# Step-wise delta-rule preparation inside the projection, and float32 attention on halves of the TensorE columns

## The chip, the cores and the metric

One core of a Trainium2 chip runs the whole program. The metric is device time in microseconds (us), the median of several executions. TensorE is the matrix engine (PE; PEld is its weight load), VectorE is DVE, ScalarE is ACT, GpSimd is POOL; SP issues most DMAs.

## The reference, cut to what matters

A two-layer decoder trunk takes 1024 prompt tokens and 8 x 8 sample tokens (1088 columns in all). The change is in layer 0, whose mixer has two parts behind one input projection:

```python
qkv, z, b_raw, a_raw, cq, ckv, kpe = jnp.split(h @ w_in, SPLIT_AB, axis=-1)
qkv = jax.nn.silu(sum(ext[:, i:i + t] * conv_w[i] for i in range(CONV_W)))
q = l2norm(q); k = l2norm(k)
o_a, s_new = gated_delta_rule(q, k, v, g, beta, s0)          # 4 heads of 128
o_b = attend(q_nope, q_pe, ckv, kpe, w_uk, w_uv)             # 8 heads
return jnp.concatenate([o_a, o_b], -1) @ w_out, new_buf, s_new, ckv, kpe
```

Per chunk of tokens and head the delta rule needs the products k k^T and k q^T times a decay, the inverse of a unit triangular matrix made of the first, and then a recurrence over chunks. Attention of the sample tokens reads 4096 cached positions for each of 8 sequences through a page table; attention of the prompt is causal over 1024 positions. Afterwards come the layer's MLP, an HGRN2 layer and a second MLP, which the change does not touch.

## The kernel before, in words

Activations lie as 128 features x 1088 columns, cut in three chunks of 384, 384 and 320 columns (`CH`). A projection tile is 8 contraction steps; operands are split in a high and a low float32r part and each step is three passes (`dense`, L334 to L336), so a tile is 24 passes for each chunk and 72 in all.

`in_proj` computes 21 such tiles: two of cq, one of rotary key and gates, two of ckv, then per delta-rule head the q, k and v tiles (kept with three earlier columns in `ext`, written to DRAM as `ext_d`) and z.

`attend_sample` runs beside it. For each of 4 pairs of sequences and 8 groups of 4 pages, `scores` loads the transposed latent of each sequence (`la`), splits it in high and low parts (ACT copies, DVE subtracts) and multiplies; high and low parts of the query lie in columns 0 to 63 and 64 to 127, so two halves are added afterwards (L801, L802). `mix` transposes the probabilities (L829), gathers the latent rows (`lt`, an indirect DMA that POOL issues), splits them too and multiplies (L850). A ninth small group holds the new tokens.

`prompt_prep` (32 tiles of 512 columns, two contraction steps of three passes) makes the prompt's keys, values and queries. Then `gdn_heads` runs four heads in two streams (0 and 2; 1 and 3). `ready(h)` loads `ext_d`, does the convolutions (L949, L952), SiLU, norms (L966, L969), decays (L978 to L987) and products (L996, L997), then waits until the head before is inverted, inverts its triangular matrices with 32x32 tiles (L1027) and prepares the recurrence; `recur(h)` is the recurrence (L1178 to L1197) and the output norm (L1206). `attend_prompt` is woven with it: `scores` makes softmax rows of one head and 128 queries, `mix` transposes and splits the probabilities of 256 queries and multiplies them with V, whose high and low parts fill the 128 columns (L1385), and adds the halves. When the heads are done, `out_early` takes five of the eight output-projection rows, and after attention `out_late` the rest.

The generators are merged by `weave`, which takes the stream with the least cost so far; a scheduler then orders each engine's instructions by that order as priority and by what is ready in a simulated timeline. Waits on tile buffers and on PSUM banks come from the pools: `WT`, `BK`, `BP`, `GB` and `LA` hold stream weights, bank counts and buffer counts.

Of the kernel before, what the change touches and what calls it, by code (L numbers as in the profile page):

```python
# [19 lines left out]
NT = 1088  # L20
# [15 lines left out]
def shape_constants():  # L36
# [31 lines left out]
    t = np.arange(64) % 8  # L68
    smk = np.full((128, 8, 64), 0.0, np.float32)
    for bb in range(8):  # L70
        col = np.arange(64)
        ok = (col[None, :] // 8 == bb) & (col[None, :] % 8 <= t[:, None])
        smk[:64, bb] = np.where(ok, 0.0, NEG)
# [3 lines left out]
def lay_out(I):  # L77
# [3 lines left out]
    A["cst"], A["rope"], A["rope2"], A["smk"] = c, rope, rope2, smk.reshape(128, 512)  # L81
# [55 lines left out]
    kr = f("cache_mla_krope")[0].reshape(NPOOL, 1, 2, 64, 32).transpose(0, 1, 2, 4, 3)  # L137
    kr = np.broadcast_to(kr, (NPOOL, 2, 2, 32, 64)).reshape(NPOOL, 128, 64)
# [188 lines left out]
def dense(k, acc, w, xs, kk_n, first=True, last=True):  # L327

    nc = k.nc
    wh, wl = w  # L330
    for kk in range(kk_n):
        xh, xl = xs[kk]
        f, l = first and kk == 0, last and kk == kk_n - 1
        nc.tensor.matmul(acc, wh[:, kk], xh, start=f, stop=False)  # L334
        nc.tensor.matmul(acc, wh[:, kk], xl, start=False, stop=False)  # L335
        nc.tensor.matmul(acc, wl[:, kk], xh, start=False, stop=l)  # L336

# [85 lines left out]
def in_proj(k):  # L423
# [3 lines left out]
    k.ext_d = k.dr.tile([4, 3, 128, 1115], F32, name="ext_d")  # L427
    k.z_d = k.dr.tile([4, 128, NT], F32, name="z_d")
    k.cq_d = k.dr.tile([2, 128, NT], F32, name="cq_d")
    xp_cm = k.P("xp", side="right")  # L430
# [32 lines left out]
    def tile(w, c):  # L463
        p = k.mm()
        dense(k, p[:, :CH[c][1]], w, xs[c], 8)
        return p

    def proj(evac, steps=None):
# [3 lines left out]
        for c, (t0, n) in enumerate(CH):  # L472
            p = tile(w, c)
# [158 lines left out]
    nc.sync.dma_start(cvi, A["sconv"])  # L632
    for h in range(4):
        for part in range(3):
# [14 lines left out]
            yield from proj(evac, None if k.keys_ready else two(ckvn))  # L649
# [4 lines left out]
            nc.sync.dma_start(k.ext_d[h, part], ext)  # L654
        z = E(f"z{h}")
        yield from proj(evac_to(z))
        nc.sync.dma_start(k.z_d[h], z[:, :NT])
    nc.sync.dma_start(O["conv"], cvo)
    xp_cm.__exit__(None, None, None)


GY = 3
# [3 lines left out]
def attend_sample(k):  # L666
# [8 lines left out]
    la_t = lambda name: T([128, 1280], name, tag="la", bufs=LA)  # L675
# [14 lines left out]
    cksh, cksl = T([128, 2, 64], "cksh", F32R), T([128, 2, 64], "cksl", F32R)  # L690
    ltsh, ltsl = T([64, 256], "ltsh", F32R), T([64, 256], "ltsl", F32R)
    kso = T([128, 64], "kso", F32R)
    idb, smb = T([128, 128], "idb", BF16), T([128, 8, 64], "smb", BF16)

    def own_keys():
        cks = la_t("cks")[:, 0:128].rearrange("p (l t) -> p l t", t=64)
        nc.sync.dma_start(cks, O["latn"].rearrange("l p n -> p l n")[:, :, SEQ:NT])
        split_pair(k, cksh, cksl, cks)
# [3 lines left out]
        split_pair(k, ltsh, ltsl, p[0:64, 0:256])  # L702

        k4 = la_t("k4")[:, 0:64]
        nc.gpsimd.memset(k4, 0.0)
        for j in range(2):
            nc.sync.dma_start(k4[64 * j:64 * j + 32, :], O["kpr"][:, SEQ:NT])
        nc.scalar.copy(kso, k4)
        nc.vector.tensor_tensor(kso[64:96, :], k4[64:96, :], kso[64:96, :].bitcast(F32), ALU.subtract)
        nc.vector.tensor_copy(idb, k.ident)  # L710
        sml = la_t("sml")[:, 0:512]
        nc.scalar.dma_start(sml, A["smk"])
        nc.vector.tensor_copy(smb.rearrange("p b t -> p (b t)"), sml)
# [14 lines left out]
    ql = T([128, 2, 8, 2, 64], "ql", F32R)  # L728
# [6 lines left out]
    for l in range(2):  # L735
# [3 lines left out]
        d = lambda j: ql[:, l, :, j, :].rearrange("p b (h t) -> p b h t", t=8)  # L739
        nc.scalar.copy(d(0), bht(p))  # L740
        nc.vector.tensor_tensor(d(1), bht(p), d(0).bitcast(F32), ALU.subtract)
        yield 1

    qr = T([128, 2, 8, 2, 64], "qr", F32R)
    zz = T([128, 1], "zz")
    nc.vector.memset(zz, 0.0)
# [3 lines left out]
    for a in range(2):  # L750
        for r in range(4):
            o = slice(32 * r, 32 * r + 32)
            if r % 2 == a:
                d = lambda j: qr[o, a, :, j, :].rearrange("p b (h t) -> p b h t", t=8)
                nc.scalar.copy(d(0), bht(p[o]))
                nc.vector.tensor_tensor(d(1), bht(p[o]), d(0).bitcast(F32), ALU.subtract)
            else:
                nc.scalar.copy(qr[o, a].rearrange("p b j t -> p (b j t)"), zz[o].broadcast_to([32, 1024]))
    yield 1

    flat = lambda w: w.rearrange("p a t -> p (a t)")
    Sx, mg, sg = {}, {}, {}
    held = deque(maxlen=8)

    def scores(pr, g):
# [5 lines left out]
        for j in range(2):  # L771
            b = 2 * pr + j
            p = k.sc()
            if g < 8:
                la = la_t(f"la{pr}{g}{j}").rearrange("p (i n) -> p i n", n=320)
# [3 lines left out]
                for i, pg in enumerate(pgs):  # L779
                    held.append(nc.sync.dma_start(la[:, i], A["latT"][bass.ds(pg, 1)].rearrange("o p n -> (o p) n")))  # L780
                lh = T([128, 4, 256], f"lh{pr}{g}{j}", F32R, tag="lh", bufs=LH)
                ll = T([128, 4, 256], f"ll{pr}{g}{j}", F32R, tag="ll", bufs=LH)
# [118 lines left out]
    yield 1  # L901


LA = 4
LH = 3


# [664 lines left out]
GB = [2]  # L1572
# [371 lines left out]
```

## Time and profile before

| | before |
|---|---|
| median of 3 runs | 3364.34 us (3357.28 to 3365.59) |
| the profiled execution | 3368.05 us, of which 3366.0 us are its span |
| PE, DVE, ACT, POOL busy | 3191.1, 1987.2, 1306.1, 560.3 us |
| mean granted TensorE clock | 0.967 |

The span runs from the first to the last instruction. A busy PE is one with any pass in its pipeline, whose ends are modelled: how fast it works is read from the distance of starts.

### The profile page before, as it was taken

Reading aid. Unit: us, or ns where it says so; the run is one execution under the profiler, and the core shown is the slowest. Engines: PE = TensorE matmul, PEld = TensorE weight load, DVE = VectorE, ACT = ScalarE, POOL = GpSimd, SP = SyncE. Lnnn points to the kernel's source line nnn. Section 1 sums busy time; section 2 is a strip of 40 time slices with the busy share of each in tenths; the row PEclk is TensorE's granted clock in tenths of the full one; section 3 lists DMA queues with packets and bytes.
Section 4 is the critical chain, followed back from the end, with each engine's and each line's share of the span. In section 5 each row is a group of like instructions: output and inputs, shape, how many; then the busy total and the mean of one; then the engine's idle time right before and its main releaser. Section 6 shows DMA issues by size and latency. Waiting matters only on the chain.

```text
span 3366.0 us, 63206 instructions
## 1 busy us (share of the span) xinstructions
PE 3191.1 (95%) x26180; PEld 3034.3 (90%) x26180; DVE 1987.2 (59%) x3511; ACT 1306.1 (39%) x2293; POOL 560.3 (17%) x536
## 2 busy tenths in 40 slices
PE   8999977888999999999999999999989999999997
PEld 7899966766888999999999888888879999999997
DVE  5788787667675544544455666555566444444456
ACT  5566674556453322112211544445535221122212
POOL 3022242102201100000000344544432000000002
PEclk9999988888889999999999999999989999999999
DMA  4687775022032111111111211111232111011111
GB/s 146 207 262 246 231 260 182 23 79 63 25 133 84 38 51 45 39 43 51 44 44 42 88 53 53 53 60 52 82 102 71 39 51 45 32 51 51 44 38 54
DMA packets 128687, 282.41 MB, mean 84 GB/s; under 512 B 14192, under 2 KB 76848, under 8 KB 128400
## 3 DMA queue, kind: packets, MB, share of 16 engines
q1 hardware_dynamic: 106656, 204.24, 18.3%
q10 hardware_dynamic: 12528, 40.58, 3.7%
q0 software_dynamic: 9216, 33.56, 3.2%
q8 instruction: 205, 3.36, 0.4%
q14 instruction: 82, 0.67, 0.1%
HBM read 233.42 MB, written 44.90 MB: 83 GB/s over the span
## 4 chain that ended last, share of the span: by engine, by line
PE 68%; DVE 5%; ACT 5%; POOL 3%; issue 2%; DMA 1%; SPq 0%; ACTq 0%; DVEq 0%; POOLq 0%
PE mm L335 11%; PE mm L334 11%; PE mm L336 11%; PE sm L1620 7%; PE sm L1622 7%; PE sm L1621 7%; PE po L1385 1%; PE tr L1394 1%; POOL y L1774 1%; DVE x L1770 1%; POOL y L1773 1%; DVE xl L318 1%; PE sm L1756 1%; POOL qg L1822 1%; PE sc L1359 1%
## 5 line engine op out<-in xcount | busy, mean ns | idle before, releaser
L334 PE MATMUL mm<-xh,wh 128*128 128x384 f32 (+1 forms) x2808 | 929.2, 331 | 12.5 <-ACT wh L265 11.0
L336 PE MATMUL mm<-xh,wl 128*128 128x384 f32 (+1 forms) x2808 | 926.5, 330 | 1.1 <-issue 0.9
L335 PE MATMUL mm<-xl,wh 128*128 128x384 f32 (+1 forms) x2808 | 925.6, 330 | 0.6 <-issue 0.6
L1623 DVE TENSOR_TENSOR xr<-xr,sm 128x384 f32<-128x384 f32 (+1 forms) x768 | 404.8, 531 | 433.1 <-PE sm L1622 433.0
L334 PEld LDWEIGHTS mm<-xh,wh 128*128 128x128 f32 x2808 | 530.0, 189 | 17.2 <-ACT wh L265 11.0
L336 PEld LDWEIGHTS mm<-xh,wl 128*128 128x128 f32 x2808 | 530.0, 189 | 4.8 <-issue 1.1
L335 PEld LDWEIGHTS mm<-xl,wh 128*128 128x128 f32 x2808 | 529.8, 189 | 4.3 <-issue 1.1
L1620 PE MATMUL sm<-hh,dh 128*128 128x384 f32 (+1 forms) x1536 | 504.5, 328 | 6.6 <-DVE xr L1623 5.2
L1622 PE MATMUL sm<-hh,dl 128*128 128x384 f32 (+1 forms) x1536 | 502.8, 328 | 0.0
L1621 PE MATMUL sm<-hl,dh 128*128 128x384 f32 (+1 forms) x1536 | 502.2, 327 | 0.0
L286 POOL TENSOR_TENSOR ssa<-ssa,ssq 128x384 f32<-128x384 f32 (+1 forms) x90 | 94.9, 1055 | 1751.0 <-ACT ssq L284 1748.0
L1597 ACT ACTIVATE hraw<-hraw 128x384 f32<-128x384 f32 (+1 forms) x192 | 96.9, 505 | 693.7 <-DVE hraw L1596 693.7
L1620 PEld LDWEIGHTS sm<-hh,dh 128*128 128x128 f32 x1536 | 288.6, 188 | 9.7 <-DVE xr L1623 7.5
L1621 PEld LDWEIGHTS sm<-hl,dh 128*128 128x128 f32 x1536 | 288.6, 188 | 0.5
L1622 PEld LDWEIGHTS sm<-hh,dl 128*128 128x128 f32 x1536 | 288.6, 188 | 0.0
L265 ACT CAST dh<-dr 128x1024 fp32r<-128x1024 f32 x64 | 66.9, 1048 | 385.7 <-PE sm L1621 381.2
L1596 DVE SCALAR_TENSOR_TENSOR hraw<-mm,rb 128x384 f32<-128x384 f32 (+1 forms) x192 | 102.7, 535 | 182.3 <-PE mm L336 182.2
L266 DVE TENSOR_TENSOR hl<-hraw,hh 128x384 fp32r<-128x384 f32 (+1 forms) x192 | 102.4, 533 | 114.9 <-ACT hh L265 114.9
L265 ACT CAST wh<-wr 128x1024 fp32r<-128x1024 f32 x96 | 100.6, 1048 | 122.0 <-PE mm L335 118.6
L266 DVE TENSOR_TENSOR wl<-wr,wh 128x1024 fp32r<-128x1024 f32 x96 | 121.0, 1262 | 43.0 <-ACT wh L265 43.0
L841 POOL DMA_INDIRECT lt<-in_lat,ix x64 | 70.8, 1106 | 187.4 <-DVE ltl L266 170.0
L265 ACT CAST hh<-hraw 128x384 fp32r<-128x384 f32 (+1 forms) x192 | 95.0, 495 | 5.1
(755 smaller groups left out, 5404.1 us busy)
## 6 DMA issues: line engine op xcount, KB each, us to landing
la<-in_latT SPq DMA_DIRECT2D x256, 160.0 KB
wr<-in_w_up SPq DMA_DIRECT2D x64, 512.0 KB
dr<-in_w_down ACTq DMA_DIRECT2D x64, 512.0 KB
wr<-in_w_in_c SPq DMA_DIRECT2D x32, 512.0 KB
win<-in_w_in_ab SPq DMA_DIRECT2D x21, 512.0 KB
ext_d<-ext SPq DMA_DIRECT2D x12, 557.5 KB
oC_d<-g SPq DMA_DIRECT2D x8, 544.0 KB
q_d<-q SPq DMA_DIRECT2D x16, 256.0 KB
```

The source lines that it names most:

```text
L265: k.nc.scalar.copy(hi, src)
L266: (eng or k.nc.vector).tensor_tensor(lo, src, hi.bitcast(F32), ALU.subtract)
L286: nc.gpsimd.tensor_tensor(acc, acc, t, ALU.add)
L334: nc.tensor.matmul(acc, wh[:, kk], xh, start=f, stop=False)
L335: nc.tensor.matmul(acc, wh[:, kk], xl, start=False, stop=False)
L336: nc.tensor.matmul(acc, wl[:, kk], xh, start=False, stop=l)
L1596: nc.vector.scalar_tensor_tensor(raw[:, s], p[:, :n], 0.0, k.rb[:, s], ALU.max, ALU.mult)
L1597: nc.scalar.activation(raw[:, s], raw[:, s], AF.Square)
L1620: nc.tensor.matmul(p[:, :n], wh[:, m], hh[:, s], start=a, stop=False)
L1621: nc.tensor.matmul(p[:, :n], wh[:, m], hl[:, s], start=False, stop=False)
L1622: nc.tensor.matmul(p[:, :n], wl[:, m], hh[:, s], start=False, stop=b)
L1623: nc.vector.tensor_tensor(k.xr[c][:, m], k.xr[c][:, m], p[:, :n], ALU.add)
```

## The change

Three parts. First, convolutions, SiLU, norms, decays and key products of each head are made during `in_proj`: two generators, `conv` and `pairs`, are put in a queue, and after contraction steps 2, 4 and 7 of every chunk (`RK`) one step of the queue is emitted. The results (`y_d`, `U_d`, `A_d`) go to DRAM in place of `ext_d`, and `ready` loads them and begins at the inversion. Second, sample attention multiplies the cached latents as float32, without splits: the two sequences of a pair use array columns 0 to 63 and 64 to 127. Third, prompt attention works on head pairs: the two heads' values fill the two halves of the columns, the probabilities are float32 and copied from PSUM once, by ACT and DVE in turn. Scores of prompt attention keep the three passes.

```diff
-def dense(k, acc, w, xs, kk_n, first=True, last=True):
+def dense(k, acc, w, xs, kk_n, first=True, last=True, between=None):
...
+        if between:
+            between(kk)
...
+    def between(kk):
+        if kk in RK:
+            step()
...
+    def conv(h, part, e, y):
+        w = lambda i: k.vec[:, V_CW + 4 * (4 * part + h) + i:V_CW + 4 * (4 * part + h) + i + 1]
+        es, ys = b11(e[:, 1027:1115]), b8(y[:, SEQ:NT])
+        nc.scalar.mul(y[:, :SEQ], e[:, 0:SEQ], w(0))
+        nc.scalar.mul(ys, es[:, :, 0:8], w(0))
+        for i in range(1, 4):
+            nc.vector.scalar_tensor_tensor(y[:, :SEQ], e[:, i:i + SEQ], w(i), y[:, :SEQ], ALU.mult, ALU.add)
+            nc.vector.scalar_tensor_tensor(ys, es[:, :, i:i + 8], w(i), ys, ALU.mult, ALU.add)
+            yield
+    def pairs(h, ys, z):
...
+        other_tables(k, scr, z[:, 0:1], [lambda t=t: nc.scalar.activation(t[:, :NT], t[:, :NT], AF.Silu) for t in (kn, q, v, z)])
+        nc.sync.dma_start(k.y_d[h, 2], v)
+        nc.sync.dma_start(k.z_d[h], z[:, :NT])
+        yield
+        items = [(t, t0, n) for t in (kn, q) for t0, n in CH]
...
+        for i in range(len(items) + 2):
+            if i > 1:
...
+                nc.scalar.activation(r[i - 2], ps[i - 2], AF.Ln, bias=k.eps[:, 0:1])
+                nc.scalar.activation(r[i - 2], r[i - 2], AF.Exp, scale=-0.5)
+                nc.vector.tensor_tensor(t[:, t0:t0 + n], t[:, t0:t0 + n], r[i - 2], ALU.mult)
+            if 0 < i <= len(items):
...
+                nc.tensor.matmul(ps[i - 1], k.ones, r[i - 1], start=True, stop=True)
+            if i < len(items):
...
+                nc.scalar.activation(r[i], t[:, t0:t0 + n], AF.Square)
+            yield
+        nc.sync.dma_start(k.y_d[h, 1], kn)
+        for c0, c1 in ((0, 4), (4, 8), (8, 9)):
...
+                nc.tensor.matmul(V(p)[:, c - c0], gg[0:m, c, h:h + 1].broadcast_to([m, 128]), tri, start=True, stop=True)
+            yield
...
+                nc.vector.scalar_tensor_tensor(V(dd)[0:m, c - c0], V(p)[0:m, c - c0], nb[0:m, c, h:h + 1], mk, ALU.add, ALU.min)
+            nc.scalar.activation(eg[:, :m * nu], p[:, :m * nu], AF.Exp)
+            nc.scalar.activation(dd[0:m, :m * nu], dd[0:m, :m * nu], AF.Exp)
...
+            yield
+            p1, p2 = k.mm(), k.mm()
+            for src, p in ((kn, p1), (q, p2)):
+                for c in range(nu):
...
+                    nc.tensor.matmul(V(p)[0:m, c], kn[:, s], src[:, s], start=True, stop=True)
+            yield
+            for p, n, dst in ((p1, "u", k.U_d), (p2, "a", k.A_d)):
...
+                nc.vector.tensor_tensor(t[0:m, :m * nu], p[0:m, :m * nu], dd[0:m, :m * nu], ALU.mult)
+                nc.sync.dma_start(dst[h, 0:m, c0:c1, 0:m], V(t)[0:m])
+            nc.gpsimd.tensor_tensor(q[:, hs], q[:, hs], eg[:, :m * nu], ALU.mult)
+            yield
+        nc.sync.dma_start(k.y_d[h, 0], q)
...
-            nc.sync.dma_start(k.ext_d[h, part], ext)
+            ys.append(rp.tile([128, NT], F32, tag="qkv"[part], name=f"y{h}{part}"))
+            work.append(conv(h, part, ext, ys[-1]))
...
+        yield from proj(evac_to(z), None, between)
+        work.append(pairs(h, ys, z))
...
+    while step():
+        yield 1
+RK = [2, 4, 7]
...
@@ attend_sample, scores: per pair and group, no splits @@
+            for l in range(2):
+                for j in range(2):
+                    nc.tensor.matmul(p[half(j)], ql[:, l, 2 * pr + j], las[j][:, :, 128 * l:128 * l + 128], start=l == 0, stop=False)
+            for a in range(4):
+                for j in range(2):
+                    nc.tensor.matmul(pv[half(j), :, 32 * a:32 * a + 32], qr[:, a, 2 * pr + j], las[j][:, :, 256:288], start=False, stop=a == 3)
+            nc.scalar.copy(S, p)
...
@@ attend_sample, mix @@
+        (nc.vector.tensor_copy if g % 2 else nc.scalar.copy)(P4[0:kp, 0:n], p.rearrange("p (i t) -> p i t", t=128)[0:kp, 0:n])
...
+        for r in range(n):
+            for j in range(2):
+                nc.tensor.matmul(po[half(j), 0:256], P4[0:kp, r, half(j)], xs[j][:, r] if g < 8 else lts,
+                                 start=g == 0 and r == 0, stop=g == 8)
-LA = 4
-LH = 3
+LA = 5
...
@@ gdn_heads, ready: loads in place of convolutions to products @@
+        nc.sync.dma_start(U[:, 0:8], k.U_d[h, :, 0:8])
+        nc.sync.dma_start(kn[:, :NT], k.y_d[h, 1])
+        nc.sync.dma_start(vc[:, :NT], k.y_d[h, 2])
+        nc.sync.dma_start(Ai[:, 0:8], k.A_d[h, :, 0:8])
+        nc.sync.dma_start(qc[:, :NT], k.y_d[h, 0])
...
@@ attend_prompt, mix @@
+            for a in range(m):
+                for j in range(2):
+                    nc.tensor.matmul(po[half(j), 0:128], V[:, kb + a, half(j)], t[:, j, a], start=kb + a == 0, stop=kb + a == qb)
...
+            (nc.scalar.copy if turn[0] % 2 else nc.vector.tensor_copy)(t[:, :, 0:m], p[:, :, 0:m])
...
-WT = [1, .5, 1.5, 0]
-BK = [2, 2, 2]
+WT = [1, 1.3, 1.5, 0]
+BK = [3, 2, 2]
-GB = [2]
+GB = [1]
```

The sample's page rows shrink from 320 to 288 columns, since each rotary key lies there once and `qr` holds zeros in the rows of the other quarters.

## Rows read from the trace of the kernel before

**Rows 1.** The page's first line.
```profile
span 3366.0 us, 63206 instructions
```

**Rows 2.** By stage: start:end, length, busy PE, PEld, DVE, ACT, POOL, clock, DMA share, GB/s.
```profile
25.00:449.00 424.00, 410.54 (x2516) 388.24 (x2515) 323.55 (x503) 262.12 (x426) 96.20 (x119) 0.98 0.70 222
449.00:557.00 108.00, 90.16 (x478) 74.34 (x477) 74.08 (x104) 61.11 (x107) 38.02 (x29) 0.89 0.58 199
557.00:613.00 56.00, 33.61 (x613) 24.40 (x611) 40.41 (x71) 33.26 (x58) 15.37 (x21) 0.66 0.39 128
613.00:970.00 357.00, 325.18 (x5366) 271.33 (x5364) 244.50 (x657) 192.90 (x473) 59.83 (x84) 0.90 0.19 61
...
1113.00:3366.00 2253.00, 2188.40 (x16435) 2141.48 (x16433) 1197.84 (x1993) 674.64 (x1068) 322.46 (x250) 0.99 0.16 53
```

**Rows 3.** Groups by line and shape, 0 to 557 us: busy, mean ns.
```profile
L266 DVE TENSOR_TENSOR ltl<-lt,lth 128x1024 fp32r<-128x1024 f32 x64 | 86.5, 1357 | 16.6 <-ACT lth L265 13.3 <-issue 1.2 <-PE po L850 1.2
L266 DVE TENSOR_TENSOR ll<-la,lh 128x1024 fp32r<-128x1024 f32 x64 | 79.4, 1241 | 22.5 <-ACT lh L265 21.2 <-issue 0.8
L802 DVE TENSOR_TENSOR S<-sc,S 64x512 f32<-64x512 f32 x64 | 43.5, 680 | 1.0
```

**Rows 4.** Timeline of PE, sample attention: start, length, passes (xcount).
```profile
300.78 0.63 PE L829 MATMUL tr<-cst,S 128*128 128x128 f32 x4
...
302.25 0.40 PE L790 MATMUL sc<-ll,ql 128*128 128x512 f32 x1
302.49 0.40 PE L792 MATMUL sc<-kh,qr 128*128 128x256 f32 x2
302.73 0.34 PE L336 MATMUL mm<-xh,wl 128*128 128x384 f32 x1
```

**Rows 5.** Timeline of PE where float32 passes fall on both column halves.
```profile
543.94 0.46 PE L896 MATMUL tr<-oL,uvs 128*64 128x64 f32 x8
544.33 0.91 PE L966 MATMUL g<-U,cst 128*128 128x384 f32 x2
545.08 1.06 PE L978 MATMUL g<-cst,gg 128*128 128x128 f32 x8
```

**Rows 6.** Timeline of PE, float32 passes on one half between projection passes.
```profile
1963.42 0.33 PE L336 MATMUL mm<-xh,wl 128*128 128x384 f32 x1
1963.60 0.34 PE L334 MATMUL mm<-xh,wh 128*128 128x384 f32 x1
1963.87 1.15 PE L1802 MATMUL sm<-y 128*64 128x64 f32 x16
1964.94 0.44 PE L335 MATMUL mm<-xl,wh 128*128 128x384 f32 x1
1965.22 0.34 PE L336 MATMUL mm<-xh,wl 128*128 128x384 f32 x1
```

**Rows 7.** Chain that ended last, 557 to 613 us: start, length, what.
```profile
564.69 7.47 DMA A<-ext_d
...
611.21 1.29 DVE q L969
```

**Rows 8.** Waits of 175 to 449 us: us in total, times, longest.
```profile
POOL lt L841 <- DVE ltl L266: 134.5, 38, 9.8
...
POOL ext L638 <- DMA ext_d<-ext: 15.9, 4, 5.5
```

**Rows 9.** First inversion passes of the heads (tile um): duration, first and last start.
```profile
L1027 PE MATMUL g<-cst,um x144: 191/191/213, 575.7 to 867.9; 32*32 32x32 f32 x144
...
L1027 PE MATMUL mm<-cst,um x144: 191/224/255, 643.2 to 791.5; 32*32 32x32 f32 x144
```

**Rows 10.** Last passes of each prompt item (line L1416): duration min/median/max, first and last start.
```profile
L1416 PEld LDWEIGHTS po<-cst,pm x128: 132/137/231, 583.9 to 1050.3; 128*64 128x64 f32 x128
L1416 PE MATMUL po<-cst,pm x128: 272/273/476, 583.9 to 1050.4; 128*64 128x128 f32 x128
```

**Rows 11.** Output norm of the heads (line L1206), last row of its passes.
```profile
L1206 PE MATMUL mm<-q,cst x10: 432/486/590, 727.7 to 968.6; 128*128 128x384 f32 x8, 128*128 128x320 f32 x2
```

## What was predicted

> **What bounds the kernel now.** I read the page first [rows 1], then busy time by stage, then single stages as timelines and chains. By stage [rows 2] everything after 1113 us is untouched. Up to 449 us the projection and the sample attention keep PE busy for 411 of 424 us at a clock of 0.98; from 449 to 557 us, while the prompt's keys, values and queries are made, PE is busy for 90 of 108; from 557 to 613 for 34 of 56 at a mean clock of 0.66, so the lower of its two levels (1.2 and 2.4 GHz) for much of it; then at 0.90 to 970.
>
> Busy time flatters PE, so I counted work: passes times the distance of their starts. A projection pass of 384 columns takes 0.175 us [rows 6], one of 320 by that 0.147, so 21 tiles x 72 passes are 251 us. A pair and group of the sample: eight passes of 512 at 0.24 and four of 256 at 0.12 for the scores, four transposes at (0.63 - 0.28) / 3 = 0.117 and sixteen passes of 256 at 0.12 for the values [rows 4], together 4.79; 32 of them are 153. Prompt preparation, 192 passes at 0.235, is 45. With some 35 for norms, set-up and the first of the heads' preparation I get about 484 us of work in the first 557. From 557 to 970 the same count over all lines (attention 119, inversion and recurrence 115, the heads' preparation and the rest 29) gives only about 263 us of work in 413: an estimate, but far enough below to say that here not PE's rate sets the time but the heads' chain. The reader sees that in the chain from 557 to 613 [rows 7]: `ext_d` loaded for 7.5 us, then convolution, SiLU, norm piece by piece on ACT and DVE until 611, with little on PE. Heads 2 and 3 pay it again: their inversions start at 791 and 868 where those of heads 0 and 1 start at 576 and 643 [rows 9].
>
> **The change part by part.** The profiled execution took 3368.05 us (3366.0 its span, 2 around it), 3.7 above the median; the sum is made against it.
>
> *Sample attention's PE work.* One question decides: do float32 passes on the two column halves run together? A float32 matmul is two instructions here, 0.112 us each for 128 columns (eight in 1.06 us, the last one's length 0.28 taken off, [rows 5]). Eight passes of 64 columns on both halves start within 0.46 - 0.22 = 0.24 us, 34 ns apart [rows 5]; sixteen on one half start (1.15 - 0.22) / 15 = 62 ns apart [rows 6]. So halves overlap nearly wholly at 64 columns; no row shows it at 256 or 512. Together: scores 2 x 2 pairs of passes at 4 x 0.112 = 0.448, plus 4 x 2 at 0.112, 2.69 us; mix 0.47 + 8 x 0.224 = 2.26; 4.95 in all. One after the other: 2.69 x 2 + 0.47 + 3.58 = 9.43. I take together, by [rows 5], the nearest.
> Between passes of the full array a batch on halves costs more: [rows 6] the sixteen occupy 1.07 us where 16 x 0.062 is 0.99, their start comes 0.27 after a pass of 0.175, and the projection's first pass 0.28 before the next. That is 0.08 + 0.095 + 0.105, some 0.3 us a batch, two batches a group: 0.6. So 5.55 against 4.79, +0.76 x 32 = **+24 us** of PE work; serial, 10.03 - 4.79 = 5.24 x 32 = +168.
>
> *Splits.* DVE loses `ltl`, `ll` and the halves' sum, 86.5 + 79.4 + 43.5 = 209 us [rows 3], ACT the copies before them, about as many. They were beside PE, so their going is worth nothing in itself; but the wait of POOL's gathers for `ltl` (134.5 us, [rows 8]) goes. What is late next is the buffer itself: `la` and `lt` share five, a group needs four, and they are now held until PE has read them. Four buffers are 2 x 590 + 2 x 524 KB = 2.23 MB, 10 us at the 222 GB/s of the stage [rows 2]: 36 groups fit in the some 390 us they have, without much to spare.
>
> *Head preparation.* Moved, not removed: per head six norm matmuls (two passes of 0.34 us by 384 x 0.112 / 128), 9 decays and 18 products (two of 0.112), 4.0 + 2.0 + 4.0 = 10 us of PE, 40 for four, of which about 8 ran before 557 already: **+32 us** in the first part. DVE's convolutions and the rest (some 90 us) and ACT's (some 75) lie beside the projection, covered by the 209 just freed; without that cover DVE, busy for 324 of 424 us [rows 2], would be full and the projection would wait for its evacuations. Queues: SP issues about 36 transfers more (nine per head); SP has room, but the `la` loads stand behind them. On POOL the gather issues wait for buffers, and the new copies of `eg` and the q product stand behind these; q's store waits for them, and q, k, v have one buffer each, so the next head's convolution waits for that store (5.5 us is the longest such wait now, [rows 8]).
>
> *First part, sum.* 24 + 32 = 56 us more work in a part that has 557 - 484 = 73 us without any, 14 of them in the first 25 us, some 33 from 449 to 557, where DVE's and ACT's relief shortens the splits' chain. I let 33 be absorbed: **prompt attention and the first inversion start 23 us later, at 580.** Ends: all absorbed 0; none +56.
>
> *Heads and prompt attention, 557 to 970.* The chain's pieces of preparation go: 48 us from 564.7 to 612.5 [rows 7], about 40 and 50 for the later heads, partly run beside another head's recurrence: 0 to 138 us. Work in the stretch is 263 - 24 (preparation) = 239, plus mode changes of the values: 80 batches for 32 before, 48 x 0.3 = 14. At the stage's rate now (263 / 413 = 64%) 253 take 397 us, -16; if the heads go at their present pace without preparation, the first inversion starts 17 us sooner after 557's counterpart (575.7 - 557, less 2), and the last one some 225 us after it, where it is 292 now [rows 9] (70, 85 with the recurrence between, 70): -84. The idle stretch of [rows 7] gone and one copy for each transposed block in place of copy and subtract speak for denser work; I take 350 us, 72%: **-63 us**. V's passes on halves cost what they did: per block 4 x 0.112 / 2 for two heads against 2 x 0.12, if together.
>
> *After.* `out_early` starts when the heads are through (968.6 now, [rows 11]) and attention ends 82 us later (1050.4, [rows 10]). I keep that distance: 0.
>
> Sum +23 - 63 = **-40**: 3368 - 40 = 3328, less 3.7 for the median: **3325 us**, 1.2% below 3364.
>
> **Weight loads.** The passes of [rows 6] follow at 62 ns although each has a weight load of about 137 ns [rows 10], so here loads ran under passes of the same half; and eight passes in 0.24 us [rows 5] leave no room for eight waits. A chain of load and pass is the second rival. The Trainium skill ("TensorE: Matmul & The Clock Gate", The mechanism) says that a weight load overlaps running matmuls only where the row groups differ, and the two halves share all rows: by the rows the sum stays 3325, by that rule it would be that rival's 3413. By that rule the trace does not agree.
>
> **The rivals.**
> 1. *Halves do not overlap for long passes* (the other side). The sample gets 168 - 24 = 144 us dearer on the bound engine: 3325 + 144 = 3469. It decides from a pair of passes that takes 1.25 times one: 40 / 32 = 1.25 us a group on 4.95. For: no row at 512 columns. Against: [rows 5]. Chance 0.08.
> 2. *Each pass waits for its weights.* 20 pairs of passes a group (12 for scores, 8 for values) x 0.137 [rows 10] x 32 = 88 us: 3413. Against: [rows 5, 6]. Chance 0.03.
> 3. *The first part absorbs nothing.* PE full until the projection ends, the last head's 21 steps left with no projection beside them, stalls at the single q, k, v buffers (3 x 5.5 = 16): start at 557 + 56 + 16, 49 later than forecast: 3374. It decides when the first inversion starts after 620 (557 + 63), where all is given back. For: five buffers, one queue of steps. Against: DVE and ACT have room. Chance 0.17.
> 4. *Attention, not the heads, sets the end.* From 583.9 to 1050.4 its 32 items go at 15 us each [rows 10]; if that is its own chain of softmax and transposes, it only starts 23 us later: 3388. Against: that pace was kept beside the heads' passes, and its copies halve. Chance 0.10.
> 5. *The heads' chain falls by the whole.* -84, and the first part 15 later: 3368 - 69 - 4 = 3295, down to 3280 if the first part is not later. Chance 0.20.
>
> **Numbers.** The forecast, 3300 to 3350, has the remaining 0.42. The range 3275 to 3390 leaves out rivals 1 and 2 (0.11) and some 0.08 at the edges. What this measurement can tell from no change is 0.3%, 10 us: faster is below 3354, slower above 3374. Faster: 0.42 + 0.20 and 0.04 of rivals 3 and 4, 0.66. Same: 0.09 of rival 3 and 0.03 of rival 4, 0.12. Slower: 0.11 + 0.06 + 0.05, 0.22.
>
> **What would show it.** Right: sample passes on halves in pairs, a pair of 512 columns every 0.45 us; DVE in the first 557 us far below 400 us busy; the first inversion passes [rows 9] at 570 to 600 with the next head's at once behind; the heads' last norm [rows 11] near 930; mean clock from there on above 0.90. Wrong: pairs spaced 0.9 us (rival 1); inversion start after 620 (3); attention's last item more than 100 us after the heads' end (4). The least sure step is the density of 72%.

## The result and the profile after

The changed kernel takes 3331.06 us (median of 4 runs, 3327.91 to 3337.41), the kernel before beside it 3361.24 (3357.28 to 3365.59): a ratio of 0.990, 95% interval 0.988 to 0.992. 3325 was predicted, with 3300 to 3350 for the forecast's own case; the fall is 30 us where 39 was forecast from a median of 3364. The profiled execution, first on the page of the changed kernel, then as busy time by stage (start:end, length, busy PE, PEld, DVE, ACT, POOL, clock, DMA share, GB/s):

```profile
span 3332.2 us, 63550 instructions
...
PE 3203.8 (96%) x26796; PEld 2962.6 (89%) x26796; DVE 1712.8 (51%) x3100; ACT 1099.6 (33%) x1990; POOL 531.5 (16%) x549
```

```profile
25.00:497.00 472.00, 469.80 (x3051) 375.12 (x3051) 189.43 (x354) 171.03 (x312) 87.19 (x134) 1.00 0.58 189
497.00:598.00 101.00, 92.17 (x512) 64.91 (x509) 38.33 (x64) 40.89 (x87) 43.22 (x47) 0.95 0.83 286
598.00:624.00 26.00, 17.86 (x109) 12.86 (x107) 16.98 (x44) 12.04 (x30) 7.56 (x13) 0.75 0.89 294
624.00:938.00 314.00, 305.18 (x6042) 243.94 (x6042) 181.72 (x517) 132.24 (x370) 46.49 (x71) 0.95 0.24 76
938.00:1060.00 122.00, 105.28 (x585) 99.98 (x584) 64.90 (x103) 45.28 (x81) 15.84 (x15) 0.93 0.30 94
...
1060.00:3332.00 2272.00, 2201.53 (x16459) 2155.13 (x16457) 1205.67 (x2002) 679.75 (x1077) 321.19 (x253) 0.98 0.16 52
```

The edges are events: last projection pass (427 before, 496 now), end of prompt preparation (557, 598), first inversion (576, 624), last output norm of the heads (970, 938), last pass of the late output projection (1109, 1060). [Rows 2] cuts otherwise at two of them: 449 is where prompt preparation starts (542 now), and 613 lies behind the first inversion. So the projection ends 69 us later, and the preparation of the prompt is made in 57 us instead of 108. The span's 33.8 us less are four numbers:

| from | to | before | after | difference | predicted |
|---|---|---|---|---|---|
| start | prompt preparation made | 557 | 598 | +41 | +23 |
| there | last output norm of the heads | 413 | 340 | -73 | -63 |
| there | last pass of the late output projection | 139 | 122 | -17 | 0 |
| there | end of the span | 2257 | 2272 | +15 | 0 |

The same events as rows, to set beside [rows 9 to 11]: first inversion passes of the heads (duration, first and last start; both banks' names), last output norm, last passes of the prompt attention's items.

```profile
L1040 PE MATMUL g<-cst,um x216: 191/194/257, 668.4 to 827.6; 32*32 32x32 f32 x108
...
L1040 PE MATMUL mm<-cst,um x72: 236/236/258, 624.4 to 625.3; 32*32 32x32 f32 x72
...
L1213 PE MATMUL g<-q,cst x4: 432/434/445, 822.6 to 938.0; 128*128 128x320 f32 x4
...
L1420 PE MATMUL po<-cst,pm x128: 272/273/421, 608.2 to 930.3; 128*64 128x128 f32 x128
```

In the kernel before, the last norm pass stands in the row of the other bank, which [rows 11] doesn't show:

```profile
L1206 PE MATMUL g<-q,cst x14: 432/484/561, 721.6 to 969.8; 128*128 128x384 f32 x8, 128*128 128x320 f32 x6
```

So the heads ended at 970 and not at 968.6. Their inversions now start at 624 for the first, 668 for the second and 827 for the last, 203 us after the first, where it was 292. From first inversion to last norm it is 314 us, where it was 394. And attention, which ended 81 us after the heads, now ends 8 us before them.

The sample's passes on column halves, in the timeline of PE (start, length, passes):

```profile
216.13 1.50 PE L867 MATMUL sc<-la,ql 128*64 128x512 f32 x5
...
235.30 1.95 PE L914 MATMUL po<-lt,P 128*64 128x256 f32 x16
...
302.14 1.50 PE L867 MATMUL sc<-la,ql 128*64 128x512 f32 x5
303.06 0.60 PE L871 MATMUL sc<-la,qr 128*64 128x128 f32 x4
303.48 0.59 PE L867 MATMUL sc<-la,ql 128*64 128x512 f32 x1
303.91 1.04 PE L871 MATMUL sc<-la,qr 128*64 128x128 f32 x12
304.87 0.45 PE L335 MATMUL mm<-xh,wh 128*128 128x384 f32 x1
305.16 0.34 PE L336 MATMUL mm<-xl,wh 128*128 128x384 f32 x1
305.33 0.33 PE L337 MATMUL mm<-xh,wl 128*128 128x384 f32 x1
```

Five passes of 512 columns start within 1.50 - 0.59 = 0.91 us: two pairs and the next pass. Read pass by pass, the two of a pair start 7 ns apart and the next pass on the same half 429 to 430 ns after the one before it (480 behind the first pair of a batch), so a pair takes what one takes, 0.43 us where 0.45 was worked out; the sixteen passes of 256 columns start 7 ns and 209 ns apart in turn. Rival 1 falls here. Two further things are to be seen. From 303.06 on the halves are out of step: four passes of 128 on one half run beside one of 512 on the other, and still both halves work. And the projection's first pass behind a batch holds 0.28 us, 304.874 to 305.158 read pass by pass, where the others hold 0.17.

### The profile page after: what moved, and what is told of

It reads as the page before. It is cut to its first block, busy times and chain, and to the rows that moved or that the text cites. A ratio compares the mean times of both kernels' runs of the same rounds, so it can differ in the third digit from the quotient of the medians.

```text
span 3332.2 us, 63550 instructions
## 1 busy us (share of the span) xinstructions
PE 3203.8 (96%) x26796; PEld 2962.6 (89%) x26796; DVE 1712.8 (51%) x3100; ACT 1099.6 (33%) x1990; POOL 531.5 (16%) x549
## 5 line engine op out<-in xcount | busy, mean ns | idle before, releaser
L910 POOL DMA_INDIRECT lt<-in_lat,ix x64 | 63.3, 990 | 196.6 <-PE sc L871 119.5
```

## The experiments

Each kernel was timed beside the kernel before; the ratios are to that. The kernel before took 3361 to 3370 us from one set of runs to the next, so between sets the ratios compare and not the medians. "First, second and third part" are the three parts of the change as numbered ahead.

| kernel | median us | ratio | 95% interval |
|---|---|---|---|
| whole change (first set) | 3331.06 | 0.9898 | 0.9879 to 0.9916 |
| whole change again | 3329.55 | 0.9882 | 0.9860 to 0.9904 |
| second part alone (`s_only`) | 3382.62 | 1.0041 | 1.0024 to 1.0057 |
| third part alone (`a_only`) | 3367.19 | 0.9996 | 0.9980 to 1.0011 |
| without the first (`no_p`) | 3366.82 | 0.9996 | 0.9979 to 1.0012 |
| without the third (`no_a`) | 3320.42 | 0.9860 | 0.9835 to 0.9885 |
| without the third, again | 3324.36 | 0.9872 | 0.9852 to 0.9893 |

The theory to be tested was the prediction's: the gain is head preparation out of the heads' chain, the float32 sample attention costs some PE time, and the prompt attention only helps the density with one copy a block. The rivals: the move is a wash (preparation costs as much in the first part as it saves later), and the gain comes from DVE's and ACT's relief.

**Second part alone.** Sample attention as in the change; head preparation and prompt attention as before.

```diff
-                split_pair(k, lh, ll, la[:, :, 0:256])
...
+            for l in range(2):
+                for j in range(2):
+                    nc.tensor.matmul(p[half(j)], ql[:, l, 2 * pr + j], las[j][:, :, 128 * l:128 * l + 128], start=l == 0, stop=False)
...
-BK = [2, 2, 2]
+BK = [3, 2, 2]
```

> Only the sample attention of the change (float32 on column halves, with its buffer, bank and weight settings); the heads' preparation and the prompt attention as before. My theory: PE pays 24 to 30 us more in the first part, of which the idle time from 449 to 557 us absorbs most, and nothing is gained later: 3350 to 3375, no change that 0.3% can tell; DVE's busy time in the first 557 us falls by about 200 us without a gain. Rival (the split copies on ACT and DVE were what delayed the first part, so their going is the gain): 3325 to 3340, with the prompt's preparation done 20 us or more earlier than 557.

It is slower, by 0.4%, a little more than the theory's "no change". Its busy time by stage, to the projection's end and from there to the end of prompt preparation:

```profile
25.00:460.00 435.00, 434.55 (x2849) 352.39 (x2848) 114.46 (x217) 91.94 (x183) 72.18 (x116) 0.99 0.62 199
460.00:568.00 108.00, 94.10 (x517) 65.88 (x515) 51.97 (x79) 51.57 (x95) 38.45 (x32) 0.92 0.72 244
```

Up to the end of prompt preparation DVE falls from 397.63 us (323.55 + 74.08, [rows 2]) to 166.43, ACT from 323.23 to 143.51, and yet that end comes 11 us later, most of the 13 us lost; up to the projection's end, at 460 instead of 427, PE is busy for all but 0.45 us. The splits were beside PE: taking them away gave nothing. That the gain is this relief of the vector engines falls here. The run has the change's banks, buffers and stream weight, and doesn't tell them from the float32 passes.

**Third part alone.** Values on column halves of a head pair, one copy for each transposed block; the rest as before.

```diff
-                    nc.tensor.matmul(po[:, fs[a]], V[:, kb + a], t[:, a, fs[a]], start=kb + a + i == 0, stop=kb + a + i == nk)
+                    nc.tensor.matmul(po[half(j), 0:128], V[:, kb + a, half(j)], t[:, j, a], start=kb + a == 0, stop=kb + a == qb)
...
-                nc.vector.tensor_tensor(d(lo), pp, d(hi).bitcast(F32), ALU.subtract)
+            (nc.scalar.copy if turn[0] % 2 else nc.vector.tensor_copy)(t[:, :, 0:m], p[:, :, 0:m])
```

> Only the prompt attention of the change (head pairs on column halves, one copy a block). My theory: the heads' chain is as long as before (last norm near 960 to 970 us), attention ends with it and not 80 us later, and the early output projection then runs alone: 10 to 20 us less than before, 3340 to 3352. Rival (attention's copies alone set the pace from 557 us on, so that this part brings the whole gain): 3325 to 3333, heads through by 935. Rival (attention is only filler): 3361.

No change that can be told, so the theory's 10 to 20 us are not there, and "attention is only filler" stands. Last passes of the attention's items and of the heads' output norm:

```profile
L1413 PE MATMUL po<-cst,pm x128: 272/273/421, 581.3 to 940.6; 128*64 128x128 f32 x128
...
L1206 PE MATMUL g<-q,cst x14: 432/486/590, 736.0 to 983.0; 128*128 128x384 f32 x8, 128*128 128x320 f32 x6
```

Attention ends 110 us sooner than in [rows 10], at 940.6, but the heads end at 983.0, 13 later than before (969.8). They are what the early output projection waits for, so an attention that is through sooner buys nothing while the heads are not.

**Without the first part.** Second and third part, with head preparation left in `ready`.

```diff
-            work.append(conv(h, part, ext, ys[-1]))
+            nc.sync.dma_start(k.ext_d[h, part], ext)
...
-        work.append(pairs(h, ys, z))
+        nc.sync.dma_start(k.z_d[h], z[:, :NT])
```

> Both float32 attentions, but the heads' preparation (convolutions to key products) left where it was, after the prompt's preparation. My theory: the sum of the two single parts, 3335 to 3360, and slower than the whole change by what the shorter chain of the heads brings less what its work costs in the first part: 10 to 25 us above 3331. Rival (moving the preparation is a wash: what it takes from the chain it adds to the projection): the same as the whole change, 3331.

3366.82, no change from the kernel before, and some 35 us above the whole change by the ratios, where the theory had 10 to 25. First inversions and last output norm:

```profile
L986 PE MATMUL g<-cst,um x72: 191/191/212, 580.8 to 581.5; 32*32 32x32 f32 x72
...
L1165 PE MATMUL g<-q,cst x8: 432/466/590, 734.3 to 973.5; 128*128 128x384 f32 x4, 128*128 128x320 f32 x4
```

The heads take 393 us here, as before the change (394), and 314 with the preparation moved. Between this kernel and the whole change lies the whole gain; that the move is a wash falls.

**Without the third part.** First and second part with the old prompt attention, twice: alone, and in a later set of runs beside the whole change.

```diff
-                    nc.tensor.matmul(po[half(j), 0:128], V[:, kb + a, half(j)], t[:, j, a], start=kb + a == 0, stop=kb + a == qb)
+                    nc.tensor.matmul(po[:, fs[a]], V[:, kb + a], t[:, a, fs[a]], start=kb + a + i == 0, stop=kb + a + i == nk)
```

> Sample attention and the moved preparation, prompt attention as before. My theory: first part as in the whole change (preparation of the prompt done at about 598 us), the heads' chain shorter by 40 to 60 us than before, attention ending some 60 to 80 us after the heads: 3345 to 3360, that is 15 to 30 us above the whole change. Rival (the heads' chain alone sets the end, attention follows it): 3331 to 3336.

> First and second part (head preparation in the projection, sample attention in float32 on halves) with the old prompt attention, timed beside the whole change. Theory 'the third part takes time from the heads' chain': in the first look the heads' output norm ended at 906 us here and at 938 in the whole change, while the late output projection ended at 1062 and 1060, so the ends are equal and the whole change and this kernel agree within 0.3%. Rival 'the third part costs time': the medians of the first look, 3320 against 3331, hold side by side as well: faster than the whole change by 8 us or more, ratio 0.986 to the kernel before.

> The changed kernel as it is, timed beside the same kernel without its third part. Every theory expects 3331 us give or take 7, a ratio of 0.990 to the kernel before; it is the measure for the two kernels that follow it here.

In the first set neither expectation held: 3320.42 is not 15 to 30 us above the whole change, and not level with it, but below. Side by side 3324.36 (3320.5 to 3327.8) and 3329.55 (3321.0 to 3333.9): 5 us, with intervals that overlap for most of their width. The second profile of this kernel, last output norm and last item of attention:

```profile
L1213 PE MATMUL g<-q,cst x4: 432/432/435, 789.9 to 904.3; 128*128 128x320 f32 x4
...
L1423 PE MATMUL po<-cst,pm x128: 269/273/476, 612.5 to 1011.0; 128*64 128x128 f32 x128
```

With the old attention the heads are through at 904, in 282 us, and attention trails until 1011; with the new one the heads take 314 and attention is through with them. The late output projection ends at 1062 in the one and at 1054 to 1060 in the other. The third part thus moves work from behind the heads to beside them, and the end of the stage hardly moves. In neither set is it worth anything; if it changes the time, it costs a few us.

**Attention held behind the heads.** The whole change, with the weight of the prompt attention's stream raised.

```diff
-WT = [1, 1.3, 1.5, 0]
+WT = [1, 1.3, 2.5, 0]
```

> The whole change with the prompt attention's stream weight at 2.5 instead of 1.5, so that its passes stand behind those of the heads in the order. Theory 'the new attention is dense enough to hold up the heads, and what it wins it loses there': the heads' output norm ends by 915 us instead of 938, attention later than 930 and beside the early output projection again, the late output projection at 1050 to 1060: 3318 to 3331 us. Rival 'the heads wait for themselves, not for attention's passes': the output norm stays within 8 us of 938.

3322.57 us, ratio 0.9871 (0.9851 to 0.9892): 7 us below the whole change beside it, not told apart from it. The last norm comes at 922, 16 sooner, neither by 915 nor within 8 of 938, so between the two theories. First of the changed kernel, then of this one, the timeline of PE where the early output projection begins (in brackets the idle time before, and what ended it):

```profile
937.76 0.71 PE L1213 MATMUL g<-q,cst 128*128 128x320 f32 x2
949.95 1.60 PE L335 MATMUL mm<-o0h,woh 128*128 128x384 f32 x4 [11.47 <-ACT o0h L265]
```

```profile
935.75 1.12 PE L1400 MATMUL po<-PT,V 128*64 128x128 f32 x8 [1.85 <-DVE PT L1410]
936.66 0.64 PE L1420 MATMUL po<-cst,pm 128*64 128x128 f32 x4
937.73 1.59 PE L335 MATMUL mm<-o0h,woh 128*128 128x384 f32 x4 [0.43 <-ACT o0h L265]
```

Whenever the heads end, some 11 to 16 us pass before the last head's output has come back from DRAM and is split. Attention's last items used to cover that time; in the changed kernel they are gone by then and PE stands idle for 11.47 us; held back, they cover it again.

**Halves one after the other in the order.** In the sample's passes the loop over the two sequences goes outside, so that one half's passes stand together in the program.

```diff
-            for l in range(2):
-                for j in range(2):
+            for j in range(2):
+                for l in range(2):
...
-        for r in range(n):
-            for j in range(2):
+        for j in range(2):
+            for r in range(n):
```

> The changed kernel with one thing turned round: in the sample attention all matmuls of one sequence come first and then those of the other, so that neighbours in the program lie on the same half of the columns. Same work, same operands. My theory (only neighbours on different halves stream together, and the order of the program decides it): a group of the sample goes from about 5 to 9.4 us of PE, 4.4 x 32 = 140 us, so 3430 to 3475. Rival (the passes are brought together again whatever the order, or the halves never were what set the pace): 3331 within 15.

3367.46 us (10 runs), ratio 1.0004 (0.9986 to 1.0022): the whole gain is gone, 36 us, but not the 144 us that passes one after the other would cost by rival 1's working. The timeline of PE shows why:

```profile
226.50 0.64 PE L867 MATMUL sc<-la,ql 128*64 128x512 f32 x1
226.52 0.65 PE L871 MATMUL sc<-la,qr 128*64 128x128 f32 x4
226.99 0.59 PE L867 MATMUL sc<-la,ql 128*64 128x512 f32 x1
227.01 0.60 PE L871 MATMUL sc<-la,qr 128*64 128x128 f32 x4
227.41 1.02 PE L867 MATMUL sc<-la,ql 128*64 128x512 f32 x2
```

One half's passes of 512 run beside the other half's passes of 128, until one half has nothing left; from 227.41 two passes of 512 follow each other alone on one half, 1.02 - 0.59 = 0.43 us apart. In the program all four of these passes of 512 stand ahead of the eight of 128, whose first starts 13 ns after the first of the four. Overlap between halves doesn't need neighbours in the program, but it ends where the work of one half runs out. Counted by the distance of starts, the scores take 132 us instead of 109 and the values 91 instead of 69; prompt preparation ends 48 us later (646), which the heads give back in part. The four passes of 128 columns on one half start 0.11 us apart, (0.60 - 0.27) / 3, though each has a weight load of 137 ns: loads run under passes of the same half, as in [rows 6]. By the sentence of the Trainium skill that the prediction weighed ("TensorE: Matmul & The Clock Gate", The mechanism) they would be 0.25 apart, an estimate from 0.11 and 0.137; the trace doesn't agree here either. The same section of the Trainium skill also lets a load go ahead that targets the background weight buffer; no run here shows which buffer was loaded.

**The last head's steps beside prompt preparation.** The 21 steps that are left when the projection ends are woven with `prompt_prep` instead of standing in front of it.

```diff
-    while step():
-        yield 1
-    rp_cm.__exit__(None, None, None)
+    k.tail = step
...
-        yield from prompt_prep(k)
+        yield from weave((prompt_prep(k), 1, 0), (tail(), 1, 0))
```

> The changed kernel, but the last head's remaining steps (norms, decays, products after the last projection tile) are emitted beside the prompt's preparation instead of ahead of it, with their tiles in memory that the preparation does not reuse. Nothing else changes. In the changed kernel the preparation starts 45 us after the last projection pass. My theory (the last head's steps hold up the preparation, as a chain with little on PE): preparation done 15 to 25 us sooner, 3306 to 3318. Rival (PE is full in this stretch with the sample's rest anyway, so that order does not matter): 3331 within 8.

3322.19 us (3318 to 3325, 5 runs), ratio 0.9879 (0.9862 to 0.9896): 9 below the whole change in the first set, but its ratio is that of the whole change measured again, 0.9882, so nothing that can be told; neither theory nor rival is decided. Why so little is in the timeline of the changed kernel while those steps run:

```profile
509.73 0.69 PE L944 MATMUL tr<-cst,os 128*128 128x128 f32 x2 [5.50 <-ACT os L941]
...
514.72 1.49 PE L686 MATMUL mm<-nq,cst 128*128 128x384 f32 x2
516.13 4.57 PE L914 MATMUL po<-lt,P 128*64 128x256 f32 x26
520.63 1.45 PE L686 MATMUL mm<-nq,cst 128*128 128x384 f32 x4
522.02 1.08 PE L914 MATMUL po<-lt,P 128*64 128x256 f32 x6
```

The stretch from 497 to 541 isn't empty: sample passes fill it between the norms (L686), and PE is idle for 7 us of 44. With the steps beside prompt preparation the sample's passes are what remains, and the preparation ends at 590, 8 us sooner.

**Both together.** Without the third part, and with the last steps beside prompt preparation: the edits of the two kernels above.

```diff
-                    nc.tensor.matmul(po[half(j), 0:128], V[:, kb + a, half(j)], t[:, j, a], start=kb + a == 0, stop=kb + a == qb)
+                    nc.tensor.matmul(po[:, fs[a]], V[:, kb + a], t[:, a, fs[a]], start=kb + a + i == 0, stop=kb + a + i == nk)
...
-        yield from prompt_prep(k)
+        yield from weave((prompt_prep(k), 1, 0), (tail(), 1, 0))
```

> First and second part, old prompt attention, and the last head's steps no longer in front of prompt preparation but beside it. Theory 'the two savings add': the steps beside the preparation gave 9 us to the whole change, leaving out the third part 0 to 11: 3306 to 3322 us, ratio 0.983 to 0.987. Rival 'both savings fall into the same idle time': no faster than the better of the two alone, 3320 us or more.

3331.34 us, ratio 0.9896 (0.9877 to 0.9916). They don't add: this is the whole change's own time. The inversion starts 9 us sooner (613), the heads end at 905 as without the steps moved, and attention at 1016. No version tried beats the whole change by more than the measurement tells.

**The sample's stream weight.** The weight of the sample's stream beside the projection, 1.3 in the change, doubled nearly and more than halved.

```diff
-WT = [1, 1.3, 1.5, 0]
+WT = [1, 2.0, 1.5, 0]
```

> The changed kernel with the sample's weight at 2.0 for 1.3, so that the sample lags behind the projection and more of its work is left for the stretch of the last head's steps and of the prompt's preparation. My theory (PE is the bound of the first part, only idle time of that stretch can be filled): 0 to 10 us less, 3321 to 3335. Rival (the gathers' buffers bound the sample, so a later sample ends later): 3345 to 3370.

```diff
-WT = [1, 1.3, 1.5, 0]
+WT = [1, .5, 1.5, 0]
```

> The changed kernel with the sample's weight at 0.5 as before the change, so that the sample runs ahead of the projection. My theory: the sample is through before the last head's steps, PE idles there, and the first part grows by 10 to 25 us: 3340 to 3356. Rival (the weight is only a priority and PE is full all the same): 3331 within 8.

At 2.0 3342.0 us (ratio 0.9946, 0.9926 to 0.9966), at 0.5 3333.01 (0.9912, 0.9893 to 0.9931). Busy time by stage, at 2.0 from the projection's end to the end of prompt preparation, to the sample's end, to the first item of attention:

```profile
435.00:555.00 120.00, 112.72 (x645) 72.62 (x643) 36.98 (x66) 38.32 (x80) 40.66 (x40) 1.00 0.91 308
555.00:640.00 85.00, 62.12 (x1338) 41.40 (x1336) 11.92 (x30) 15.03 (x41) 32.53 (x49) 0.85 0.56 190
640.00:672.00 32.00, 23.69 (x607) 20.53 (x605) 18.46 (x32) 15.78 (x30) 2.51 (x4) 0.66 0.56 154
```

With the sample late, prompt preparation is through at 553 and the first inversion at 576, as early as before the change, but the sample runs to 640, and attention, which the program puts behind the whole sample stream, begins at 672 instead of 608; until 640 PE is busy for 62 of 85 us. That costs 0.5 to 0.6% of the time, less than the rival had. With the sample early (its end at 506 instead of 572) the preparation ends at 617, 19 us later as the theory had it, and yet the time is the same as the rival had it: from there to the last norm it is 326 us instead of 340, at a clock of 0.98 instead of 0.93. How the first part's work is ordered matters little as long as the sample isn't last.

The first part alone was not run. That its buffers have no room beside those of the old sample attention, so that the second part is what makes the first one possible, is argued and not shown.

## Why the prediction was right

Time and direction were right, and so was the place of the gain; most of the terms were mis-sized. The terms:

1. **Halves run together** (forecast against rivals 1 and 2): right, 0.43 us a pair of 512 columns. The term was +24 us of PE work. By the distance of starts the sample's passes take 196 us where they took 169 (+27), and the projection's 273 where they took 262 (+12). So it is +39: the price of a change between whole array and halves was right (0.11 us for the pass behind it), but the sample's passes come in 81 batches where two a group make 64, which at 0.28 us each is some 5 of the 15 us that are missing. The other 10 are not accounted for.
2. **Preparation moved**, +32 us of PE work in the first part: 38.5 us there now, 9.0 before, +29.5. Right.
3. **33 us absorbed**: mis-sized. From 25 us on PE was idle for 31 us of this part and is for 11 now: 20 were absorbed, and nearly nothing more was to be had (469.80 busy of 472 up to 497). The prediction's count of work came out too low; by it 59 us were free there (73, less 14 in the first 25). With items 1 and 2, and prompt preparation's own passes 5 us shorter (51 to 46 us), this makes the first part +41 instead of +23. The first inversion at 624 is past the mark of 620 from which rival 3 decides "where all is given back"; that conclusion was wrong, because the heads gave more than the forecast's -63.
4. **The splits are worth nothing in themselves**: right, by `s_only`. The wait of the gathers that was to go did not go, it changed its cause. Waits of 175 to 497 us in the changed kernel (total, times, longest):

```profile
POOL lt L910 <- PE sc L871: 98.0, 20, 12.3
...
POOL lt L910 <- PE po L914: 50.5, 20, 7.5
```

   148.5 us for 134.5 in [rows 8]: what is late next is the shared buffer, held until PE has read it, as the prediction said. It cost nothing that shows: PE is busy for 469.80 of 472 us.
5. **Heads and prompt attention, -63 by a density of 72%**: mis-sized, -73. Busy time from the end of prompt preparation to the heads' last norm, before and after:

```profile
557.00:970.00 413.00, 358.80 (x5976) 295.73 (x5974) 284.91 (x727) 226.15 (x531) 75.19 (x105) 0.87 0.22 70
```

```profile
598.00:938.00 340.00, 323.05 (x6150) 256.80 (x6149) 198.70 (x561) 144.28 (x400) 54.05 (x84) 0.93 0.29 93
```

   PE is busy for 87% and 95%. The prediction's 263 us of work and 64% were far too low, so they did not prove that only the heads' chain sets the time here. Of the 36 us of work that went, 37 are the preparation (the prediction took off 24, where its own 40 - 8 gives 32), attention's values and other passes are 16 less, its transposes and scores, which now lie wholly in the stretch, 13 more, and the heads' own passes 4 more. The other 37 are idle time. The mechanism, chains of preparation out of the way and denser work, was right, and without the new attention beside them the heads are 30 us faster still. Rival 5 comes near (-84), but not by its pieces: the last inversion comes 203 us after the first, sooner than its 225; the first one comes 26 us behind the prompt's preparation where it was 18, and not 17 sooner, since the products have to be loaded back first (timeline of POOL):

```profile
612.91 1.75 POOL L1024 COPY uc<-U 32x256 f32<-32x256 f32 x4 [6.62 <-DMA U<-U_d]
```

   The estimate that V's passes cost what they did was wrong: 61 us before, 45 after. The sum also leaves out the clock. From first inversion to last norm it was 0.88 before, is 0.92 without the first part, 0.95 in the changed kernel (624 to 938, above), and 1.00 in the one with the sample's weight at 0.5; here before, without the first part and at 0.5:

```profile
576.00:970.00 394.00, 349.05 (x5926) 289.02 (x5912) 268.25 (x706) 214.87 (x512) 64.18 (x90) 0.88 0.18 58
```

```profile
581.00:974.00 393.00, 353.26 (x6308) 279.70 (x6300) 251.84 (x646) 196.77 (x471) 59.18 (x89) 0.92 0.19 60
```

```profile
642.00:944.00 302.00, 289.59 (x6047) 233.39 (x6045) 178.54 (x518) 130.91 (x371) 43.49 (x71) 1.00 0.25 80
```

   Four profiles with the same heads and attention (the changed kernel twice, `j_outer`, the sample's weight at 0.5) take 314, 308, 307 and 302 us there at 0.95, 0.97, 0.99 and 1.00. By these 12 us for 0.05, an estimate, 0.88 to 0.95 is some 17 of the 80 us from 394 to 314, and 0.92 to 0.95 some 7 of the 79 between the kernel without the first part and the whole change: the larger part isn't the clock. No run tells the moved work's load on DVE and ACT from its place in the chain; the third part alone frees 19 us of DVE and 18 of ACT in this stretch, and its heads end no sooner.
6. **After, 0, attention 82 us behind the heads**: the step that failed in kind. Attention ends with the heads, its 22 us that ran behind them are gone (-17 net), but the early output projection has lost the cover for its loads (11.47 us idle).
7. **The rest, 0**: +15 in this execution. From the late output projection to the end PE makes the same 16457 passes in the same order, is busy for 2201.53 us instead of 2192.40, and the granted clock is 0.98 instead of 0.99. Most of it lies in the HGRN2 layer; first the kernel before, then the changed one, same events at both ends within 1 us (560 and 571 us):

```profile
1880.00:2440.00 560.00, 532.14 (x6213) 499.31 (x6215) 320.81 (x506) 262.98 (x364) 239.28 (x180) 0.99 0.17 59
```

```profile
1831.00:2402.00 571.00, 539.11 (x6174) 506.87 (x6172) 322.55 (x509) 264.00 (x367) 236.34 (x179) 0.97 0.17 57
```

The sum of the four is -34 where -40 was predicted: errors of +18, -10, -17 and +15, the last with no cause that the change explains. That the total came within 6 us of the prediction is partly luck: the errors cancel.

What stays open: whether the +15 belongs to the change. Over the fourteen profiled executions the time behind the late output projection goes from 2253 to 2275 us and follows the time that PE spent there at the lower of its two levels, 1.2 GHz: 36 us in the shortest, 86 in the longest, added up over the clock's steps in the trace. Both profiles of the whole change are at the long end (2272 and 2275), those without the third part but with the first at the short end (2256, 2261 and 2253); but the whole change with the last steps moved has 2259, and the second part alone, without the third, 2267. It also blurs the comparison of the last kernels, whose stages end closer together than that.

## What to carry to other kernels

Work on the vector engines that lies beside a full matrix engine was worth nothing when it was removed, and worth most of the gain where it stood in a chain that the matrix engine waits for: here 30 us of PE work moved into a stretch with PE at 99.5% still paid, because the heads behind it take 80 us less. When a trailing stream is made to end earlier, look at what it covered: here the loads of the next stage came to light. Two column halves each need work at hand, not neighbouring instructions, so give both the same amount and let neither run out.

## What was not expected of the hardware

Float32 passes on the two column halves overlap across unequal shapes (one of 512 beside four of 128), not only in equal pairs, so putting one half's passes first costs 36 us and not 144. A stretch in which PE makes the same 16457 passes in the same order took 2257 us in one profile and 2272 in another, with 50 and 76 us of it at the lower clock, and no edit near it.
